# Down projection of a gated FFN in seven block products, with earlier loads at two places ahead of it

## The chip, the cores and the metric

The kernel runs on one core of a Trainium2 chip. The metric is device time in microseconds, from one launch. The core has TensorE (matmul, "PE"; its weight loads are "PEld"), VectorE ("DVE"), ScalarE ("ACT"), GpSimd ("POOL") and SyncE ("SP", used for starting DMAs); "SPq", "ACTq" and "POOLq" are DMA issues on those engines' queues.

## The reference

One decoder layer on x of 1024 tokens by 1024 features, float32:

```
h = rmsnorm(x, norm_mix_g);  z = h @ w_in            # 1024 x 2816
y_a: short gated conv; y_b: attention, 8 heads of 64; y_c: Conformer conv (31 taps), layernorm, silu
x = x + concat(rmsnorm(y_a), rmsnorm(y_b), rmsnorm(y_c)) @ w_out
h = rmsnorm(x, norm_ffn_g)
gate, val = split(causal_dwconv(h @ w_up, conv_f_w, 3 taps))   # 2 x 2816 features
x = x + (silu(gate) * val) @ w_down                  # (1024 x 2816) @ (2816 x 1024)
return rmsnorm(x, final_g)
```

## The kernel before

Every float32 operand of a matmul is split into a rounded part `hi` (ACT copy, line 71) and a rest `lo` (a subtraction on DVE or POOL, line 72). A product is three matmuls, hi*hi, hi*lo, lo*hi (`mm3`, lines 89 to 92: L90, L91, L92), each 128x128 by 128x512. The order of TensorE's instructions is the program order, written by hand; the other engines' instructions are put in an order by the framework's planner ahead of the run, and wait on semaphores. Each engine and each DMA queue then works in that order.

The stages, in order of time:

- Front: projections of the input. `proj_qk(i, ...)` makes a 128-row block of queries (i below 4) or keys (i = 4 to 7), splits it and stores hi and lo to DRAM (`qk[i]`). Blocks 0, 4, 1, 5 are made here.
- Attention (about 235 to 445 us): 80 chunks, ten for each of 8 heads. `load_head(h)` brings a head's query, key, bias and value tiles from DRAM, most of it on POOL's queue; heads 0 and 1 are loaded after the last projection, the others one or two heads ahead. Between the attention's matmuls TensorE runs "filler" from a generator: `more_qk()` (blocks 2, 6, 3, 7, tile `f_ps`), then `out_ac()`, the part of the output projection that doesn't need attention. `out_ac()` starts with `yield 0` four times while the splits `yh`/`yl` of its activations are made, then loads the weights of the first 512 columns into tiles `wac` and the residual x on ACT's queue.
- Out projection, norm, up projection (about 530 to 929 us). The up projection already works by seven block products instead of eight: weight sums are made on POOL (L971 to L974), one loop per 128 gate and 128 value features (`main(j)`, 22 loops). Each loop stores its activations, a 128 x 1024 block (features by tokens), to DRAM as `actd[j]` (L1007). After loops 19 and 20 `early_tiles` splits the first two blocks for the down projection into the tiles of `b11` and `b21`, which are free by then.
- Down projection (from 929 us): two halves of 512 tokens; for each, 22 blocks `kt` of 128 features, and in each block 8 output banks by three matmuls. The weights `w_down[kt]` (512 KB) are loaded and split anew in each half (`wd_hi`, `wd_lo`), the activations (256 KB) are loaded from `actd` and split (`a_hi`, `a_lo`). The last three blocks of a half run bank by bank (LAG = 3), so that each bank's residual add (L1098), square (L1100) and final norm (`finish`) overlap the next bank's matmuls.

Of the kernel before, what the change touches and what calls it, by code (L numbers as in the profile page):

```python
# [36 lines left out]
def body(tc, x_t, x_n, grow, par, cst, rel, oneh, nlnc, wc, w_cols, wv, w_out, w_up, w_down, out):  # L37
# [345 lines left out]

    def proj_qk(i, pos, tmp=None):
# [11 lines left out]
        split(t[:, :S], hi, lo, G if tmp else V)  # L396
        nc.sync.dma_start(out=qk[i][0], in_=f(hi))
# [78 lines left out]
    do_norm()  # L476
    table(AF.Exp, "sqrt")
# [9 lines left out]

    def load_head(h):
        j, s = h // 2, (h % 2) * 64
        sa = a0.tile([P, S], F32R, name="sa", tag="sa", bufs=2)  # L490
        sb = a0.tile([P, S], F32R, name="sb", tag="sb", bufs=2)
        sm = a0.tile([P, S], F32R, name="sm", tag="sm", bufs=2)
        g = a0.tile([P, S], F32, name="g", tag="g", bufs=2)
        vv = a0.tile([P, TT, P], F32R, name="vv", tag="vv", bufs=2)
        for dst, src in ((sa, (qk[j][0], qk[j][0])), (sb, (qk[j][1], qk[j][1])), (sm, (qk[4 + j][0], qk[4 + j][1]))):
            for e in range(2):
                G.dma_start(out=dst[e * 64:(e + 1) * 64, :], in_=src[e][s:s + 64, :])
        fr = fs[h:h + 1, 1:1 + S]
# [17 lines left out]
    heads = {0: load_head(0), 1: load_head(1)}  # L516
# [115 lines left out]

    yh, yl = [None] * 8, [None] * 8
# [4 lines left out]
    def load_half(rows, dh, hi, lo):  # L638
# [5 lines left out]
        mark["w"] = split(raw, hi, lo, G)  # L644
# [13 lines left out]
    def out_ac():  # L658

        close(c_x)  # L660
# [41 lines left out]
        for q in range(2):  # L702
            load_row(4 + q, *wp_pair())
# [259 lines left out]
    def main(j):  # L963
# [43 lines left out]
        nc.sync.dma_start(out=actd[j], in_=cg)  # L1007
# [158 lines left out]
```

## Time and profile before

| what | value |
|---|---|
| median of 3 runs | 1184.74 us (1183.36 to 1184.91) |
| the profiled execution | 1181.71 us, of it 1179.9 us from the first to the last instruction |
| granted TensorE clock, mean | 0.984 of full speed |
| PE, PEld, DVE, ACT, POOL busy | 96%, 80%, 64%, 43%, 44% of the span |
| attention, 235 to 445 us | 210 us |
| down projection, 929 to 1173 us | 244 us |

Busy time counts a pipelined matmul from its start to its modelled end, so two matmuls overlap: a matmul's listed duration is longer than the pace at which matmuls follow each other. The pace is read as a stretch divided by the matmuls in it. The granted clock is a share of 2.4 GHz.

### The profile page before, as it was taken

The numbers are of one execution on the slowest core, as the hardware profiler recorded it, in microseconds if no ns is written. First come the engines' busy times: TensorE is split into PE (matmuls) and PEld (weight loads), VectorE is DVE, ScalarE is ACT, GpSimd is POOL, SyncE is SP. The second block draws the span as 40 slices with busy tenths as digits, with TensorE's granted clock in tenths as the row PEclk, the third lists the DMA queues.
The fourth block names the chain that finished last, engine by engine and source line by source line (L and its number), as shares of the span: only waits on it lengthen the run. The fifth ranks groups of instructions, "written<-read, shape, count | busy, mean of one in ns | idle before, by whom it ended". The sixth has DMA issues, their size and how long they took to land.

```text
span 1179.9 us, 14291 instructions
## 1 busy us (share of the span) xinstructions
PE 1138.5 (96%) x5327; PEld 943.7 (80%) x5327; DVE 757.4 (64%) x886; ACT 503.7 (43%) x798; POOL 521.3 (44%) x328
## 2 busy tenths in 40 slices
PE   9999979899979999989999999999999999999997
PEld 7888868788858887868888888888887788888886
DVE  7599965356656666796677887788778722164214
ACT  7212115256555655573444444444444432343323
POOL 4223522423222203036677777777776043334331
PEclk9999989999989999989999999999999999999999
DMA  6218214977689604223242342332423554456531
GB/s 239 86 40 234 73 53 121 309 195 166 156 236 228 143 1 161 96 102 124 78 138 89 108 141 83 133 108 90 142 89 126 169 191 158 146 188 217 171 116 72
DMA packets 59317, 162.80 MB, mean 138 GB/s; under 512 B 6232, under 2 KB 15952, under 8 KB 59248
## 3 DMA queue, kind: packets, MB, share of 16 engines
q1 hardware_dynamic: 44784, 139.27, 36.1%
q0 software_dynamic: 12160, 16.78, 7.2%
q10 hardware_dynamic: 2304, 5.83, 1.4%
q8 instruction: 42, 0.69, 0.3%
q14 instruction: 27, 0.22, 0.1%
HBM read 127.17 MB, written 34.69 MB: 137 GB/s over the span
## 4 chain that ended last, share of the span: by engine, by line
PE 83%; DVE 6%; DMA 5%; ACT 3%; issue 2%; POOL 1%; SPq 0%; ACTq 0%; DVEq 0%; POOLq 0%
PE cb L91 8%; PE cb L90 8%; PE cb L92 8%; PE d_ps L92 7%; PE d_ps L91 6%; PE d_ps L90 6%; PE ca L92 4%; PE ca L90 4%; PE ca L91 4%; PE pv_ps L581 2%; PE f_ps L90 2%; PE f_ps L92 2%; PE f_ps L91 2%; PE t_ps L550 2%; PE v L92 1%
## 5 line engine op out<-in xcount | busy, mean ns | idle before, releaser
L72 POOL TENSOR_TENSOR w_lo<-w_raw,w_hi 128x1024 fp32r<-128x1024 f32 (+2 forms) x49 | 108.7, 2220 | 204.6 <-ACT w_hi L71 204.6
L960 DVE SCALAR_TENSOR_TENSOR x<-ut,pr,x 128x1024 f32<-128x1024 f32 x88 | 147.0, 1688 | 18.8 <-ACT x L958 18.0
L72 POOL TENSOR_TENSOR wd_lo<-w_raw,wd_hi 128x1024 fp32r<-128x1024 f32 x32 | 78.4, 2454 | 163.3 <-ACT wd_hi L71 150.7
L92 PE MATMUL d_ps<-wd_hi,a_lo 128*128 128x512 f32 x336 | 131.7, 392 | 1.2 <-DVE a_lo L72 1.2
L90 PE MATMUL d_ps<-wd_hi,a_hi 128*128 128x512 f32 x336 | 131.5, 391 | 0.5 <-ACT a_hi L71 0.5
L91 PE MATMUL d_ps<-wd_lo,a_hi 128*128 128x512 f32 x336 | 131.4, 391 | 0.5 <-POOL wd_lo L72 0.5
L72 DVE TENSOR_TENSOR a_lo<-a_raw,a_hi 128x512 fp32r<-128x512 f32 x42 | 40.0, 961 | 132.4 <-ACT a_hi L71 125.3
L71 ACT CAST w_hi<-w_raw 128x512 fp32r<-128x512 f32 (+2 forms) x61 | 46.1, 764 | 138.8 <-PE v L92 23.6
L298 DVE SCALAR_TENSOR_TENSOR yc<-u,pr,yc 128x1024 f32<-128x1024 f32 x60 | 89.7, 1548 | 1.7 <-ACT yc L295 1.4
L92 PEld LDWEIGHTS d_ps<-wd_hi,a_lo 128*128 128x128 f32 x336 | 63.5, 189 | 14.6 <-DVE a_lo L72 1.5
L90 PEld LDWEIGHTS d_ps<-wd_hi,a_hi 128*128 128x128 f32 x336 | 63.5, 189 | 14.2 <-ACT a_hi L71 1.0
L91 PEld LDWEIGHTS d_ps<-wd_lo,a_hi 128*128 128x128 f32 x336 | 63.4, 189 | 13.9 <-POOL wd_lo L72 0.8
L71 ACT CAST a_hi<-a_raw 128x512 fp32r<-128x512 f32 x42 | 25.8, 620 | 111.9 <-PE d_ps L91 108.6
L958 ACT ACTIVATE x<-ut,pr 128x1024 f32<-128x1024 f32 x44 | 50.7, 1153 | 47.8 <-DVE ut L1000 32.6
L537 ACT ACTIVATE p<-p,mn 128x128 f32<-128x128 f32 (+3 forms) x64 | 49.8, 778 | 40.5 <-DVE mn L534 40.3
L1006 DVE TENSOR_TENSOR x<-x 128x1024 f32<-128x1024 f32 x22 | 46.3, 2105 | 10.6 <-ACT x L1005 10.6
L71 ACT CAST wd_hi<-w_raw 128x1024 fp32r<-128x1024 f32 x42 | 43.9, 1048 | 20.0 <-DMA w_raw<-in 20.0
L997 DVE TENSOR_TENSOR ut<-cb,yb 128x512 f32<-128x512 f32 x22 | 15.2, 690 | 56.3 <-PE cb L92 56.3
L561 DVE TENSOR_TENSOR ptl<-t_ps,pth 128x512 fp32r<-128x512 f32 x48 | 33.1, 690 | 20.6 <-ACT pth L560 20.1
L971 POOL TENSOR_TENSOR xp<-xp 128x512 f32<-128x512 f32 x11 | 21.2, 1925 | 55.2 <-DMA xp<-in 49.8
L550 PE MATMUL t_ps<-ident,p 128*128 128x128 f32 x288 | 44.4, 272 | 0.0
L534 DVE CUSTOM_DVE_ANT_0 p<-l_ps,g 128x640 f32<-128x640 f32 (+5 forms) x34 | 33.8, 995 | 15.0 <-PE l_ps L528 14.4
(405 smaller groups left out, 3319.1 us busy)
## 6 DMA issues: line engine op xcount, KB each, us to landing
w_raw<-in SPq DMA_DIRECT2D x93, 512.0 KB, 3.7
ur<-in SPq DMA_DIRECT2D x22, 512.0 KB, 3.7
xp<-in SPq DMA_DIRECT2D x22, 512.0 KB
actd<-x SPq DMA_DIRECT2D x22, 512.0 KB
a_raw<-actd SPq DMA_DIRECT2D x42, 256.0 KB, 2.8
vd<-vt SPq DMA_DIRECT2D x8, 512.0 KB
vv<-vd POOLq DMA_DIRECT2D x8, 512.0 KB, 5.4
g<-fs SPq DMA_DIRECT2D x8, 512.0 KB, 9.5
```

Of the source, the lines that this page charges most:

```text
L71: cp = A.copy(hi, src)
L72: lo_eng.tensor_tensor(out=lo, in0=src, in1=f(hi), op=ALU.subtract)
L90: T.matmul(ps, whi, xhi, start=start, stop=False, **kw)
L91: T.matmul(ps, whi, xlo, start=False, stop=False, **kw)
L92: T.matmul(ps, wlo, xhi, start=False, stop=stop, **kw)
L298: V.scalar_tensor_tensor(out=yc[i], in0=u[i][:, j:j + S], scalar=col("cwc", j * 2 + i), in1=yc[i], op0=ALU.mult, op1=ALU.add)
L534: V.tensor_tensor_reduce(out=p[:, :n], in0=ps[:, :n], in1=gq, op0=ALU.add, op1=ALU.min, scale=1.0, scalar=3e38, accum_out=mn[:, ix:ix + 1])
L537: mark["exp"] = A.activation(out=p[:, :n], in_=p[:, :n], func=AF.Exp, scale=-1.0, bias=mn[:, ix:ix + 1], accum_out=den[h // 2][:, dc:dc + 1])
L550: T.transpose(out=tp[:, i * P:(i + 1) * P], in_=p[:, kj * P:(kj + 1) * P], identity=ident)
L958: A.activation(out=c, in_=t[:, 2:], func=AF.Copy, scale=col("cwf", 2 * 44 + m))
L960: V.scalar_tensor_tensor(out=c, in0=t[:, q:q + S], scalar=col("cwf", q * 44 + m), in1=c, op0=ALU.mult, op1=ALU.add)
L1006: V.tensor_tensor(out=cg, in0=cg, in1=cv, op=ALU.mult)
```

## The change

The down projection C = A B (tokens x 2816, 2816 x 1024) is cut into 2 x 2 blocks: A by 512 tokens and 1408 features, B by 1408 features and 512 columns. Seven products of 11 feature blocks and 4 banks replace the eight. Sums of weights (T1 = B12 - B11, T3 = B22 - B12, T2 = B22 - T1) are made on POOL inside the attention, 11 times three subtractions, and stored to DRAM. Sums of activations S1 = A21 + A22 and S2 = S1 - A11 are loaded on POOL's queue, made on POOL and DVE, and stay in SBUF. Three operands are made as a product needs them, on POOL: A11 - A21 (P7), A12 - S2 (P3), T2 - B21 (P4). P1, P2 share banks x, P5, P3 share banks y. Four early blocks are made instead of two. Ahead of it: query block 0 and key block 4 stay in SBUF (not stored), and heads 0 and 1 are loaded ahead of the last front projection; the first weights of `out_ac` go into the pair of weight tiles and are asked for before the wait for the input's tiles; x comes on SP's queue. The step numbers in `SAT` and `XAT` count feature blocks, 11 to a product. `done2`, `done6`, `done7` and `done3` add a bank to the residual x3 or to a partial sum, and `done3` finishes tokens 0 to 511. The diff, cut:

```diff
+    def load_head(h):
...
+        q, k = qk[j], qk[4 + j]
+        for dst, src in ((sa, (q[0], q[0])), (sb, (q[1], q[1])), (sm, (k[0], k[1]))):
+            for e in range(2):
+                G.dma_start(out=dst[e * 64:(e + 1) * 64, :], in_=src[e][s:s + 64, :])
...
     def proj_qk(i, pos, tmp=None):
...
+        if i % 4 == 0:
+            qk[i] = hi, lo
+            return
         nc.sync.dma_start(out=qk[i][0], in_=f(hi))
...
     proj_qk(1, 9)
     do_norm()
+    heads = {0: load_head(0), 1: load_head(1)}
     table(AF.Exp, "sqrt")
     proj_qk(5, 10, (yb[2], yb[3].bitcast(F32R), yb[2].bitcast(F32R)))
...
-    heads = {0: load_head(0), 1: load_head(1)}
...
+    def weights_load(i):
+        x = tw if i < 4 else [a1.tile([P, 512], F32, name=n, tag=n, bufs=1) for n in TW]
+        for t, (r, q) in zip(x, ((i, 0), (i, 1), (i + HF, 1))):
+            nc.sync.dma_start(out=t, in_=w_down[r * P:(r + 1) * P, q * 512:q * 512 + 512])
+    def weights_add(i):
+        b11, b12, b22 = twt.pop(i)
+        G.tensor_tensor(out=b11, in0=b12, in1=b11, op=ALU.subtract)
+        G.tensor_tensor(out=b12, in0=b22, in1=b12, op=ALU.subtract)
+        G.tensor_tensor(out=b22, in0=b22, in1=b11, op=ALU.subtract)
+        for n, t in (("T1", b11), ("T3", b12), ("T2", b22)):
+            nc.sync.dma_start(out=tsum[n][i], in_=t)
...
     def out_ac():
-        close(c_x)
+        w2 = [wp_pair() for _ in range(2)]
+        for q, r in enumerate((0, 6)):
+            load_half(r, 0, *w2[q])
+        close(c_tw, c_x)
...
-                        for q in ((0, 1) if t == 0 else (t + 1,) if t < 7 else ()):
-                            nc.scalar.dma_start(out=xp2[q], in_=x_n[q * P:(q + 1) * P, :])
+                if dh == 0 and t < 6:
+                    nc.sync.dma_start(out=xp2[t + 2], in_=x_n[(t + 2) * P:(t + 3) * P, :])
...
+    TWAT = (3, 12, 21, 30, 43, 48, 53, 58, 63, 68, 73)
+        if i in TWAT:
+            weights_load(TWAT.index(i))
+        elif i - 2 in TWAT:
+            weights_add(TWAT.index(i - 2))
...
+    SRC = {"P1": ((A11,), (B11,)), "P2": ((A12,), (B21,)), "P6": ((S2,), (T2,)), "P7": ((A11, A21), (T3,)),
+           "P5": ((S1,), (T1,)), "P3": ((A12, S2), (B22,)), "P4": ((A22,), (T2, B21))}
...
+            for q in range(2):
+                early[2 * (j - FT + 3) + q] = early_tiles(2 * (j - FT + 3) + q)
...
+    def sums_load(i):
+        for x, spec in ((ss_[S1][i], A21), (t, A22), (ss_[S2][i], A11)):
+            G.dma_start(out=x, in_=quadrant(spec, i))
+    def sums_add(i, t):
+        G.tensor_tensor(out=s1, in0=s1, in1=t, op=ALU.add)
+        V.tensor_tensor(out=s2, in0=s1, in1=s2, op=ALU.subtract)
+    def down_tiles(n, kt):
...
+                    x[i] = dn.tile([P, 512], F32, name=f"{e}_raw{i}", tag=f"{e}_raw{i}", bufs=NBUF if i == 0 else 2)
+                    nc.sync.dma_start(out=x[i], in_=quadrant(spec, kt))
...
+            if len(x) > 1:
+                G.tensor_tensor(out=raw, in0=raw, in1=x[1], op=ALU.subtract)
+            split(raw, hi, lo, V)
...
+    XAT = (6, 10, 15, 19, 45, 46, 47, 48)
+    SAT = (5, 8, 11, 14, 17, 20, 22, 24, 26, 27, 28)
+    ORDER = ("P1", "P2", "P6", "P7", "P5", "P3", "P4")
+    def run(n, y, done):
+        lag = LAG if n == "P4" else 1
...
+            ops = tiles[kt] = early[kt] if n == "P1" and kt in early else down_tiles(n, kt)
+            if kt < HF - lag:
+                for t in range(4):
+                    dmm(n, y, t, kt, ops, n not in start_of)
         for t in range(4):
...
+            for kt in range(HF - lag, HF):
+                dmm(n, y, t, kt, tiles[kt], n not in start_of)
+            done(t, banks[n, t])
...
+    def done1(t, ps):
+        A.copy(p1[t], ps)
...
+    def done5(t, ps):
+        for q in HS:
+            tt(x3[4 + t][:, q], x3[4 + t][:, q], u3[t])
+        tt(x3[4 + t][:, HS[1]], ps, x3[4 + t][:, HS[1]])
+        square(4 + t, 1)
...
+    def done4(t, ps):
+        x, o = x3[4 + t], xo[t % 2]
+        if t == 3:
+            tt(o[:, HS[1]], x[:, HS[1]], gfrow[:, HS[1]], ALU.mult, G)
+        tt(x[:, HS[0]], x[:, HS[0]], ps, ALU.subtract)
+        square(4 + t, 0)
+        finish(4 + t, o if t == 3 else None)
```

## Rows read from the trace of the kernel before

**Rows 1.** Page, busy time: us, share of the span, instructions.

```profile
PE 1138.5 (96%) x5327; PEld 943.7 (80%) x5327; DVE 757.4 (64%) x886; ACT 503.7 (43%) x798; POOL 521.3 (44%) x328
```

**Rows 2.** Windows: length, busy us (xinstructions) by engine, granted clock, DMA share, GB/s.

```profile
227.00:236.00 9.00, 4.85 (x17) 3.87 (x16) 3.00 (x10) 3.19 (x6) 4.66 (x2) 0.81 1.05 339
338.00:351.00 13.00, 6.36 (x22) 4.79 (x21) 3.68 (x6) 5.21 (x9) 5.65 (x3) 0.61 0.75 244
348.00:362.00 14.00, 13.02 (x66) 10.91 (x65) 7.12 (x11) 5.56 (x10) 6.33 (x8) 0.89 1.11 387
235.00:445.00 210.00, 198.81 (x1171) 169.87 (x1169) 130.19 (x256) 118.68 (x240) 56.59 (x60) 0.98 0.64 160
560.00:900.00 340.00, 340.00 (x1502) 281.71 (x1501) 259.37 (x228) 153.41 (x217) 254.44 (x155) 1.00 0.34 112
1060.00:1160.00 100.00, 100.00 (x443) 82.85 (x442) 26.65 (x26) 30.12 (x39) 34.39 (x14) 1.00 0.48 156
```

**Rows 3.** Waits of TensorE over the span: us in total, times, longest.

```profile
PE f_ps L90 <- ACT wac_hi L71: 5.0, 1, 5.0
...
PE f_ps L91 <- POOL wac_lo L72: 1.6, 1, 1.6
...
PE d_ps L92 <- DVE a_lo L72: 1.2, 1, 1.2
```

**Rows 4.** Timeline of TensorE at three places: start, us, instruction [idle before, releaser].

```profile
231.46 0.36 PE L527 MATMUL s_ps<-sm,sa 128*128 128x256 f32 x1 [4.15 <-DMA sm<-qk]
...
343.95 0.80 PE L90 MATMUL f_ps<-wac_hi,yh 128*128 128x512 f32 x1 [5.02 <-ACT wac_hi L71]
...
346.96 0.63 PE L92 MATMUL f_ps<-wac_hi,yl 128*128 128x512 f32 x1
...
350.80 0.57 PE L90 MATMUL f_ps<-wac_hi,yh 128*128 128x512 f32 x1
...
938.26 0.39 PE L92 MATMUL d_ps<-b21h,b21l 128*128 128x512 f32 x1
939.19 0.50 PE L90 MATMUL d_ps<-wd_hi,a_hi 128*128 128x512 f32 x1 [0.54 <-ACT a_hi L71]
...
945.29 0.39 PE L91 MATMUL d_ps<-wd_lo,a_hi 128*128 128x512 f32 x1
```

**Rows 5.** Tile `d_ps`: instructions, ns min/median/max, first and last start.

```profile
L90 PE MATMUL d_ps<-wd_hi,a_hi x336: 388/389/629, 939.2 to 1172.2; 128*128 128x512 f32 x168
```

**Rows 6.** Timelines of SP's queue and of POOL at the two places ahead.

```profile
223.78 2.27 POOL L497 DMA_DIRECT2D sm<-qk  x4 [3.98 <-DMA qk<-q_hi]
...
338.63 10.83 SPq L641 DMA_DIRECT2D w_raw<-in  x4
```

**Rows 7.** Groups by line and form: count, busy us, mean ns, idle before.

```profile
L72 DVE TENSOR_TENSOR a_lo<-a_raw,a_hi 128x512 fp32r<-128x512 f32 x42 | 40.0, 961 | 132.4 <-ACT a_hi L71 125.3 <-PE d_ps L91 3.7 <-DMA w_raw<-in 3.3
...
L71 ACT CAST a_hi<-a_raw 128x512 fp32r<-128x512 f32 x42 | 25.8, 620 | 111.9 <-PE d_ps L91 108.6 <-issue 3.3
```

**Rows 8.** Timelines of POOL and DVE, alone and side by side.

```profile
612.64 1.30 POOL L72 TENSOR_TENSOR w_lo<-ur,w_hi 128x512 fp32r<-128x512 f32 x1
613.89 2.28 POOL L72 TENSOR_TENSOR w_lo<-xp,w_hi 128x512 fp32r<-128x512 f32 x1
...
612.65 2.37 DVE L1006 TENSOR_TENSOR x<-x 128x1024 f32<-128x1024 f32 x1 [0.53 <-ACT x L1005]
...
947.63 4.76 POOL L72 TENSOR_TENSOR wd_lo<-w_raw,wd_hi 128x1024 fp32r<-128x1024 f32 x2 [7.50 <-ACT wd_hi L71]
...
950.49 2.45 DVE L72 TENSOR_TENSOR a_lo<-a_raw,a_hi 128x512 fp32r<-128x512 f32 x1 [6.87 <-ACT a_hi L71]
...
1010.33 0.69 DVE L72 TENSOR_TENSOR a_lo<-a_raw,a_hi 128x512 fp32r<-128x512 f32 x1 [4.75 <-ACT a_hi L71]
```

**Rows 9.** Timeline of the last 7 us.

```profile
1173.10 0.69 DVE L1098 TENSOR_TENSOR x<-d_ps,x 128x512 f32<-128x512 f32 x1
```

**Rows 10.** Page, DMA queues: packets, MB, share of 16 engines.

```profile
q0 software_dynamic: 12160, 16.78, 7.2%
```

More of the change, by code (lines that the diff above doesn't have):

```diff
@@ L643, in load_half @@
                           .rearrange("(b p) c -> p b c", b=2))
-        mark["w"] = split(raw, hi, lo, G)
+        for q in range(2):
+            q = slice(q * 512, q * 512 + 512)
+            mark["w"] = split(raw[:, q], hi[:, q], lo[:, q], G)
     def load_row(k, hi, lo):
@@ L1021, in body @@
         if j in (FT - 3, FT - 2):
-            early[j - FT + 3] = early_tiles(j - FT + 3)
-    close(c_um, c_h2, held["xp"], c_y, c_mm)
+            for q in range(2):
+                early[2 * (j - FT + 3) + q] = early_tiles(2 * (j - FT + 3) + q)
+    close(c_um, c_h2, held["xp"], c_y, c_w, c_mm)
     c_dn, dn = pool("dn", "left")
@@ L1051, in finish, with square @@
+    def square(t, dh):
+        q = HS[dh]
+        A.activation(out=xo[t % 2][:, q], in_=x3[t][:, q], func=AF.Square,
+                     accum_out=s3[:, 2 * t + dh:2 * t + dh + 1])
     def finish(t, last):
-        x, c = x3[t % 4], slice(t, t + 1)
+        x, c = x3[t], slice(t, t + 1)
         r = s3[:, 16:][:, c]
@@ L1058, in finish @@
         V.reciprocal(out=r, in_=r)
-        for q in HS if last else (slice(0, D),):
-            if last and q == HS[0]:
+        for q in HS if last is not None else (slice(0, D),):
+            if last is not None and q == HS[1]:
                 A.activation(out=x[:, q], in_=last[:, q], func=AF.Copy, scale=r)
@@ L1105, in body, with dmm @@
-    close(c_dp, c_dn, c_h, c_w, c_pad, c_const, c_dr)
+    nc.sync.dma_start(out=gfrow, in_=grow[1:2, :].broadcast_to([P, D]))
+    banks = {}
+    def dmm(n, y, t, kt, ops, start=True):
+        if (n, t) not in banks:
+            banks[n, t] = dps.tile([P, 512], F32, name=f"d_{y}{t}", tag=f"d_{y}{t}") if start else banks[start_of[n], t]
+        ah, al, bh, bl = ops
+        ts = slice(t * P, (t + 1) * P)
+        mm3(banks[n, t], ah[:, ts], al[:, ts], bh, bl, start and kt == 0, kt == HF - 1,
+            **({} if start else {"skip_group_check": True}))
@@ new lines, in done3 @@
+    def done3(t, ps):
+        tt(x3[t][:, HS[1]], ps, x3[t][:, HS[1]])
+        square(t, 1)
+        finish(t, None)
+    def done4(t, ps):
[5 more added lines that the diff above has]
+        finish(4 + t, o if t == 3 else None)
+    run("P1", "x", done1)
+    run("P2", "x", done2)
+    run("P6", "y", done6)
+    run("P7", "x", done7)
@@ L1106, in body @@
+    run("P5", "y", done5)
+    run("P3", "y", done3)
+    run("P4", "x", done4)
+    close(c_dp, c_dn, c_h, c_pad, c_const, c_dr)
     ms.__exit__(None, None, None)
```

171 lines of the change are left out of this document (89 added, 82 removed).

## Prediction

> **What bounds the kernel now.** I read the page's busy line first: TensorE is busy for 96% of the span, every other engine for 64% or less [rows 1]. Then the windows, to see stretch by stretch whether TensorE runs without a break. In the up projection, 560 to 900 us, it is busy for 340 of 340 us at full granted clock, 1502 matmuls, 226.4 ns each; in the down projection, 1060 to 1160, 443 in 100 us, 225.7 ns [rows 2]. Some records can be missing, so I take the pace from neighbouring starts, 0.227 us (three matmuls 0.68). So there the number of matmuls is the time. Then TensorE's list of waits, for the places where it isn't. Three places touch the change [rows 3, 4]:
>
> A, from about 339 us: the first matmul of `out_ac` waits 5.0 us for `wac_hi`, the next 1.6 for `wac_lo`. After them the matmuls follow at half pace: from 346.96 to 350.80 [rows 4], while the granted clock of 338 to 351 is 0.61 [rows 2].
>
> B, 227.3 us: the first score of the attention waits 4.15 us for the DMA of head 0's keys [rows 4], and the window 227 to 236 has a clock of 0.81 [rows 2].
>
> C, 938.5 us: the first non-early block of the down projection. The last early matmul starts at 938.26, so the next was due at 938.49; it starts at 939.19, the list of waits has 1.2 us behind it for `a_lo`, and at 945.29, ten matmuls on, the pace is back [rows 3, 4].
>
> **The change part by part.** The sum is made against the profiled execution, 1181.71 us, 1.8 of them outside the span.
>
> *Matmuls.* Before: 22 blocks x 16 banks x 3 = 1056, which the tile view confirms: 336 in each of the three operations [rows 5], and two early blocks of 8 x 3 under other tile names. After: 7 products x 11 blocks x 4 banks x 3 = 924. 132 fewer by 0.2267 us: **-29.9 us**. Nothing can hide this: TensorE has no gap there [rows 2].
>
> *C, the start.* Ten matmuls take from 939.19 to 945.29, 6.1 us instead of 2.3, and start 0.7 late: 4.5 us lost [rows 4]. Four early blocks hold 48 matmuls instead of 42, which moves the need for the next block from 938.5 to 939.9. Its splits are two of 512 columns per block (ACT 0.62, DVE 0.69 each [rows 7, 8]) where one of 1024 stood. They can still come late by an engine's order, so between 0 and -4.5; I take **-3.5**, as the need comes later and the chain is shorter.
>
> *B.* Lost: 4.2 waiting, and at most 0.19 x 9 = 1.7 of clock [rows 2], 5.9 in all. POOL's four key loads are issued at 223.78, after waiting 4.0 for key block 4 to land in DRAM [rows 6], and 7.7 us later, at 231.46, the score starts [rows 4]. Without the DRAM trip the keys can be asked for when the split is done, some 7 us earlier. Next late would be the last projection's readers or the score's chain on DVE and ACT. Between -2 and -6; I take **-5**.
>
> *A.* Lost: 5.0 + 1.6 + about 2.5 at half clock (3.84 us of matmuls that would take 1.9, and two starting slow) = 9.1. The load of the weights is issued only at 338.63 [rows 6], since its raw buffers held inputs of the `yh` splits. After the change weights come first; then the fourth `yh` input is what can be late, as it now waits for a raw buffer. It is needed nine matmuls behind the first. Between -5 and -9; **-7.5**.
>
> *Sums of weights.* 33 subtractions of 128x512 at 1.30 [rows 8] = 43 us of POOL, 33 loads and 33 stores of 256 KB on SP's queue. POOL is busy 57 of 210 us in the attention, and the DMAs carry 160 GB/s [rows 2]; 17.3 MB more in 210 us add 82. DVE's work there reads mostly PSUM. Behind a POOL subtraction stand the `f_lo` splits and the head loads, a head and more ahead of use. Cover: POOL's 153 idle us; without it, up to 43. Between 0 and +4; **+0.5**.
>
> *Within the products.* A block lasts 12 x 0.2267 = 2.72 us. ACT: two splits, 1.24. DVE: two, 1.38. POOL in P7, P3 and P4: one subtraction, 1.30. Each engine has room, but DVE and POOL don't run side by side: an `a_lo` takes 0.69 alone and 2.45 beside POOL's pair of 947.63; in the up projection POOL's 1.30, DVE's 1024-column operation and another POOL one end 3.53 us after the first began (612.64 to 616.17), almost one after another [rows 8]. Laid end to end that is 1.30 + 1.38 = 2.68 of 2.72. It fits, as it does in the up projection, where both engines are busy about 255 of 340 us each and TensorE never stops [rows 2]. Four buffers let the splits run three blocks ahead, 8 us. The Trainium skill (GPSIMD Engine Reference, "Key points") says that GpSimd shares its SBUF interfaces with VectorE and contends with two-input operations; by full exclusion the three products have 2.68 of 2.72, with nothing over for the final norms in P4, which is the second rival; the trace agrees that the two take turns.
>
> DMA: quarter tiles of 0.262 MB. P1 14 (four early blocks are done), P2 22, P6 11, P7 33, P5 11, P3 22, P4 33: 146, and 33 for the activation sums; with x3 and the output 4.2 MB each, 55.3 MB in 209.5 us = 264 GB/s, against 156 before [rows 2]. The heaviest stretch is steps 4 to 28: 43 tile loads, 33 for sums, 4 of x3 (8 tiles' worth): 22.0 MB in 68 us = 324 GB/s. The trace carried 387 GB/s for 14 us [rows 2]; so it fits too, with little over. The Trainium skill (DMA: Bandwidth & Descriptors, "Issuing engines are not separate DMA queues") says that POOL's queue brings no further DMA engines; by it the 324 is one demand, as I have counted it, and no row here tests it.
>
> Boundaries: P2 overwrites P1's banks after ACT's copies, P3 adds to P5's after DVE's reads; nine matmuls, 2.0 us, lie between. A gap like C costs 4.5 with its slow clock. From 0 (the stretch 1060 to 1160 behind the change of halves runs whole) to 13.5 (three such gaps); I take **+3**, less than one.
>
> *Tail.* The last banks of P4 come every nine matmuls (2.04 us) where two took 4.08, and DVE has 0.69 for each [rows 9] plus some 1.7 for the norm: 2.4 per token block. Three blocks fall behind by 0.4: **+1** (0 to 2).
>
> Sum: -29.9 - 3.5 - 5 - 7.5 + 0.5 + 3 + 1 = **-41.4**: 1140.3. The profiled run lies 3.0 under the median of the runs shown, so 1143.3; I say **1143**. Ends: all gains whole and no cost, -29.9 - 4.5 - 6 - 9 = -49.4, 1135; with C, B and A at their small ends, two gaps and the tail at 2, -29.9 - 2 - 5 + 0.5 + 9 + 2 = -25.4, 1159.
>
> **Rivals.**
>
> 1. *The places ahead give nothing.* POOL's queue is in order; if its head loads or the fourth `yh` input are late again, A and B stay. For it: the wait on POOL in [rows 6]. Against: the DRAM trip and the late raw buffer are gone. -41.4 + 12.5 = -28.9: about 1156.
>
> 2. *DVE and POOL become the bound.* If each of the 33 blocks of P7, P3 and P4 takes POOL 1.30 and DVE twice its mean of 0.96 [rows 7], 3.22 instead of 2.72, +16.5; with POOL at 2.28 and DVE at 0.69, 3.66, +31. For it: 2.68 of 2.72 is nearly all. Against: the up projection. 1143 - 3 + 16.5 to + 31: 1157 to 1171.
>
> 3. *Slower: DMA becomes the bound.* POOL's queue moved 16.78 MB in 7.2% of 1179.9 us, 197 GB/s [rows 10]. If the stage as a whole ran at that rate, its 55.3 MB take 281 us instead of 212.5: 1143 + 68 = 1211. It decides where the rate stays under 218 GB/s (55.3 MB in 254 us). Against: 387 GB/s [rows 2].
>
> **How the numbers follow.** Forecast 0.68 (1135 to 1152), rival 1 0.12, rival 2 0.13, rival 3 0.04, something faster than all terms 0.03. Range 1134 to 1163: the forecast, rival 1 and the lower part of rival 2. A measurement of this kernel tells about 0.2%, 2.4 us, from no change. Faster: all but rival 3 and a scrap of the rest, 0.94; same 0.02; slower 0.04.
>
> **What would show it.** Right: about 924 matmuls on the down banks at 0.227; from the first to the last of them about 212 us; no wait of TensorE over 1 us at the first score and the first `out_ac` matmul, with the clock near 1.0 there; attention's other stretches as long as before. Wrong: waits of TensorE on `a_lo`, `b_lo` in P7, P3 or P4 with DVE operations of 2 us (rival 2); casts waiting for DMAs in P1 and P2, or a granted clock under 0.9 in a product (rival 3); the first score still waiting for keys (rival 1); waits on T stores or `f_lo` in the attention.

## The result and the profile after

The changed kernel takes 1192.5 us (median of 8 runs), the kernel before 1183.3 in the same session: a ratio of 1.0064, 95% interval 1.0042 to 1.0086. It is slower by 0.6%, where 1143 was forecast. The profiled execution took 1193.07 us, 1191.3 of them in the span.

The page's busy line and its chain of work that ended last, of the kernel after [rows 1]:

```profile
PE 1117.9 (94%) x5195; PEld 922.1 (77%) x5195; DVE 837.1 (70%) x1015; ACT 525.0 (44%) x872; POOL 576.7 (48%) x418
...
PE 69%; DMA 16%; DVE 7%; ACT 3%; issue 2%; POOL 2%; SPq 1%; ACTq 0%; DVEq 0%; POOLq 0%
```

There are 132 matmuls fewer, as counted, and TensorE's busy share fell. The chain now runs through DMAs for 16% of the span, 5% before. TensorE's list of waits, the longest that touch the change (total, times, longest) [rows 3]:

```profile
PE l_ps L531 <- DVE mn L538: 10.6, 3, 5.5
PE d_x L90 <- ACT b_hi L71: 10.6, 5, 7.6
PE cb L884 <- DVE b22l L72: 8.9, 1, 8.9
...
PE d_x L91 <- DVE b_lo L72: 5.4, 7, 2.1
PE tr_ps L137 <- DVE st_c L128: 4.1, 2, 3.6
```

Five lines, four places, for which the sum had +0.5 (the attention), +3 (the two in the down projection) and nothing (the fourth). To see which stage lost how much I take TensorE's timeline and read the start of the same five matmuls in every run: the first score, the first of `out_ac`, the last transpose of token block 7, the first and the last of the down projection. From here on a stage is the difference of two columns (us from the start of the profiled span). Medians are of all runs; the one of experiment 7 holds one execution of 3076.7 us, without which it is 1184.2. The starts belong to the profiled execution alone, whose own time stands in the second column: it lies 4.8 above the median in experiment 4 and 7.0 below it in experiment 10, so the starts of two kernels can differ by some us without an edit behind it.

| kernel | median | profiled | first score | `out_ac` | last transpose | down, first | down, last |
|---|---|---|---|---|---|---|---|
| before | 1183.3 | 1181.7 | 231.5 | 344.0 | 518.7 | 929.0 | 1172.7 |
| after | 1192.5 | 1193.1 | 233.4 | 354.6 | 537.0 | 949.0 | 1182.5 |
| e1 no weight sums | 1168.4 | 1172.7 | 233.5 | 340.4 | 516.6 | 929.5 | 1162.1 |
| e2 paced | 1175.0 | 1175.6 | 234.5 | 354.5 | 534.5 | 944.7 | 1164.7 |
| e3 norms spread | 1187.2 | 1184.1 | 231.9 | 355.3 | 534.4 | 946.0 | 1173.6 |
| e4 front only | 1178.3 | 1183.1 | 231.3 | 337.1 | 519.8 | 930.1 | 1173.9 |
| e5 sums' DMAs on POOL | 1175.2 | 1173.1 | 233.9 | 338.7 | 522.7 | 932.7 | 1162.5 |
| e6 sums in up projection | 1208.9 | 1208.5 | 232.8 | 338.6 | 517.9 | 968.4 | 1197.7 |
| e7 DVE's order | 1184.3 | 1180.3 | 226.7 | 345.7 | 524.0 | 938.0 | 1169.8 |
| e8 all, sums in up | 1195.8 | 1194.4 | 227.0 | 333.5 | 506.2 | 965.5 | 1183.5 |
| e9 all, sums' DMAs on POOL | 1158.6 | 1157.1 | 227.8 | 337.4 | 512.9 | 929.0 | 1146.6 |
| e10 paced on POOL | 1180.2 | 1173.3 | 229.9 | 349.2 | 531.5 | 942.1 | 1162.7 |
| e11 front, DVE's order | 1172.9 | 1172.5 | 226.5 | 333.5 | 508.6 | 921.1 | 1163.3 |
| e12 e9, sums earlier | 1160.1 | 1163.1 | 225.8 | 333.1 | 515.2 | 933.7 | 1152.6 |

So the changed kernel enters the down projection 20.0 us late instead of 12.0 early, and needs 233.5 us for it, where 924 matmuls at 0.2267 are 209.5 and the kernel before needed 243.7. There are four places.

**In the attention**, 275 to 312 us. Rows of the timeline of the kernel after, of SP, ACT, DVE and PE:

```profile
275.91 4.13 SPq L658 DMA_DIRECT2D T<-tw  x3
280.14 3.61 SPq L649 DMA_DIRECT2D tw<-in  x3
283.84 0.39 SPq L633 DMA_DIRECT2D qk<-f_hi  x1
...
291.85 0.39 SPq L142 DMA_DIRECT2D scr<-tr_r  x1
...
295.38 0.32 SPq L658 DMA_DIRECT2D T<-tw  x1
295.79 0.52 SPq L633 DMA_DIRECT2D qk<-f_hi  x1
300.16 1.15 SPq L601 DMA_DIRECT2D rden<-scr  x2
...
304.89 0.62 ACT L71 CAST f_hi<-f_t 128x512 fp32r<-128x512 f32 x1 [6.23 <-DMA qk<-f_hi]
308.38 1.23 DVE L606 TENSOR_TENSOR yb<-yb,rden 128x1024 f32<-128x1024 f32 x1 [7.43 <-DMA rden<-scr]
311.26 0.79 PE L531 MATMUL l_ps<-sm,sa 128*128 128x512 f32 x1 [5.46 <-DVE mn L538]
```

It is read from the bottom. TensorE waits 5.46 for DVE's minimum; DVE had stood 7.43 in front of the product with `rden`. `rden` (the denominators of the softmax, spread over the partitions) goes through DRAM: DVE had written its rows at 284.2, SP issued their store at 291.85, behind stores of T that wait for POOL's subtractions and loads of `tw` that wait for those stores, and the load at 300.16, when that store had landed. ACT stands 6.23 for the store of the last `f_hi`, which is in the same queue, with the next exponentials behind it.

**In the first two products**, 949 to 1010. The windows of the kernel after [rows 2]:

```profile
949.00:980.00 31.00, 23.43 (x100) 18.80 (x99) 12.74 (x16) 9.54 (x15) 13.67 (x25) 0.89 0.83 302
978.50:984.00 5.50, 5.50 (x13) 3.80 (x13) 3.61 (x4) 1.68 (x3) 3.51 (x6) 0.57 1.04 389
980.00:1010.00 30.00, 26.38 (x103) 19.64 (x102) 18.54 (x22) 15.68 (x26) 13.77 (x18) 0.95 1.02 378
...
1070.00:1100.00 30.00, 30.00 (x134) 24.84 (x133) 24.73 (x35) 12.66 (x22) 8.66 (x6) 1.00 0.53 168
```

A stretch of 30 us at full pace has 134 matmuls, as the last line shows. 949 to 1010 has 203 of the 269 that fit into 61 us: 15 us lost. Half of it is one wait, 7.6 us up to 978.5; behind it the granted clock was 0.57 for 5.5 us, in which 13 matmuls ran, about 2.5 us more than at the pace. The timeline of the same kernel shows who is late:

```profile
959.21 0.32 SPq L1114 DMA_DIRECT2D a_raw<-actd  x1
959.74 0.54 POOL L1099 DMA_DIRECT2D S<-actd  x1 [7.60 <-DVE a_lo L72]
960.80 2.13 POOL L1099 DMA_DIRECT2D S<-actd  x4
...
970.11 0.33 SPq L1114 DMA_DIRECT2D b_raw<-in  x1
970.60 0.54 POOL L1099 DMA_DIRECT2D S<-actd  x1 [0.49 <-DMA S<-actd]
...
977.83 0.62 ACT L71 CAST b_hi<-b_raw 128x512 fp32r<-128x512 f32 x1 [7.06 <-DMA b_raw<-in]
978.50 0.80 PE L90 MATMUL d_x<-b_hi,a_hi 128*128 128x512 f32 x1 [7.57 <-ACT b_hi L71]
```

POOL has nothing that makes it wait for the products, so it issues loads for sums of later steps as fast as earlier ones land, and the quarter of w_down that TensorE needs next, issued at 970.11, is split 7.7 us later.

**In the last product**, 1151 to 1175. The timeline of the kernel after:

```profile
1151.20 7.96 DVE L1141 SCALAR_TENSOR_TENSOR x<-x,s,gfrow 128x1024 f32<-128x1024 f32 x4
...
1160.75 1.70 SPq L1142 DMA_DIRECT2D out_dram<-x  x2
1161.49 0.50 PE L91 MATMUL d_x<-b_lo,a_hi 128*128 128x512 f32 x1 [2.09 <-DVE b_lo L72]
1162.54 1.16 SPq L1114 DMA_DIRECT2D a_raw<-actd  x1
1168.51 0.62 ACT L71 CAST a_hi<-a_raw 128x512 fp32r<-128x512 f32 x1 [7.57 <-DMA a_raw<-actd]
```

The four norms of token blocks 0 to 3, which P3 ends, stand on DVE in one piece, 8 us beside POOL's subtractions. The splits come behind them, and SP, which waits for the norms with their output, issues the last loads behind 2 MB of output.

**At 207 and 526 us** (in the kernel before, and in the texts below, 202 and 507), in lines that the diff doesn't touch: `tr_ps` waits 3.6 for `st_c`, `cb` 8.9 for `b22l`. In the kernel before, the waits of `cb` there come to 4.1, none of them for `b22l`. The order that the planner gave DVE is another one at both (experiments 4 and 7). At 526 a norm stands in front of the split that TensorE waits for, as DVE's timeline of the kernel after shows:

```profile
523.03 2.28 DVE L872 SCALAR_TENSOR_TENSOR xp<-xp,rcol,g2row 128x1024 f32<-128x1024 f32 x1
525.24 0.68 DVE L72 TENSOR_TENSOR b22l<-cb,b22h 128x512 fp32r<-128x512 f32 x1
```

### The profile page after: what moved, and what is told of

Same layout as the page of the kernel before. It is cut to its first block, busy times and chain, and to the rows that moved or that the text cites. A ratio compares the mean times of both kernels' runs of the same rounds, so it can differ in the third digit from the quotient of the medians.

```text
span 1191.3 us, 14741 instructions
## 1 busy us (share of the span) xinstructions
PE 1117.9 (94%) x5195; PEld 922.1 (77%) x5195; DVE 837.1 (70%) x1015; ACT 525.0 (44%) x872; POOL 576.7 (48%) x418
## 4 chain that ended last, share of the span: by engine, by line
PE 69%; DMA 16%; DVE 7%; ACT 3%; issue 2%; POOL 2%; SPq 1%; ACTq 0%; DVEq 0%; POOLq 0%
PE cb L90 8%; PE cb L91 8%; PE cb L92 8%; PE ca L92 4%; PE ca L90 4%; PE ca L91 4%; DMA b_raw<-in 2%; PE d_y L90 2%; PE d_y L91 2%; PE d_y L92 2%; DMA scr<-tr_r 2%; PE d_x L91 2%; PE d_x L92 2%; PE d_x L90 2%; DMA f_lo<-in 1%
## 5 line engine op out<-in xcount | busy, mean ns | idle before, releaser
L72 POOL TENSOR_TENSOR w_lo<-w_raw,w_hi 128x512 fp32r<-128x512 f32 (+2 forms) x51 | 107.9, 2120 | 160.4 <-ACT w_hi L71 160.3
L90 PE MATMUL d_x<-b_hi,a_hi 128*128 128x512 f32 x160 | 64.3, 402 | 10.6 <-ACT b_hi L71 10.6
L72 DVE TENSOR_TENSOR b_lo<-b_raw,b_hi 128x512 fp32r<-128x512 f32 x73 | 60.3, 826 | 16.9 <-ACT b_hi L71 16.9
L91 PE MATMUL d_x<-b_lo,a_hi 128*128 128x512 f32 x160 | 64.7, 404 | 5.4 <-DVE b_lo L72 5.4
L92 PE MATMUL d_x<-b_hi,a_lo 128*128 128x512 f32 x160 | 63.5, 397 | 0.0
L71 ACT CAST b_hi<-b_raw 128x512 fp32r<-128x512 f32 x73 | 45.0, 616 | 20.4 <-DMA b_raw<-in 15.0
L90 PE MATMUL d_y<-b_hi,a_hi 128*128 128x512 f32 x132 | 51.5, 390 | 0.7 <-DVE x L1187 0.7
L91 PE MATMUL d_y<-b_lo,a_hi 128*128 128x512 f32 x132 | 51.4, 389 | 0.0
L92 PE MATMUL d_y<-b_hi,a_lo 128*128 128x512 f32 x132 | 51.4, 389 | 0.0
L90 PEld LDWEIGHTS d_x<-b_hi,a_hi 128*128 128x128 f32 x160 | 30.9, 193 | 19.2 <-ACT b_hi L71 12.7
```

Of the source, the lines that this page charges most:

```text
L71: cp = A.copy(hi, src)
L72: lo_eng.tensor_tensor(out=lo, in0=src, in1=f(hi), op=ALU.subtract)
L90: T.matmul(ps, whi, xhi, start=start, stop=False, **kw)
L91: T.matmul(ps, whi, xlo, start=False, stop=False, **kw)
L92: T.matmul(ps, wlo, xhi, start=False, stop=stop, **kw)
```

## The experiments

**1. Without the weight sums.** The down projection reads quarters of w_down where T1 to T3 stood, so the output isn't the reference's.

```diff
-        if i in TWAT:
-            weights_load(TWAT.index(i))
-        elif i - 2 in TWAT:
-            weights_add(TWAT.index(i - 2))
...
-    T1, T2, T3 = ((tsum[n], 0, 0) for n in ("T1", "T2", "T3"))
+    T1, T2, T3 = (w_down, 0, 0), (w_down, HF, 0), (w_down, 0, 1)
```

> Leaves out the sums of weights: no loads, subtractions or stores of T in the attention; the down projection reads quarters of w_down where it read T1 to T3, so its transfers and its arithmetic stay in number, and the output is not the reference's. Theory 1 (the T traffic stands in SP's in-order queue in front of the stores and loads that the attention waits for, f_hi and rden): the delays that the changed kernel gathers at 274 to 337 us (16 us) and at 407 (3.7) go, 20 us: about 1173, with TensorE's waits for mn and t_ps under 2 us each. Rival (the order that the planner gave DVE and the early weights of out_ac cause them): under 5 us, 1188 or more.

1168.4 us, ratio to before 0.9879 (0.9856 to 0.9903): 24 us less than the changed kernel. From the first score to the first down matmul it takes 696.0 us instead of 715.6. The down projection is as long as before the edit, 232.6. So the sums, put at +0.5, cost about 20 where they are made.

**2. The down projection's other loads paced by SP.**

```diff
-        for x, spec in ((ss_[S1][i], A21), (t, A22), (ss_[S2][i], A11)):
-            G.dma_start(out=x, in_=quadrant(spec, i))
+        with tc.issue_after(mark["ld"].ins):
+            for x, spec in ((ss_[S1][i], A21), (t, A22), (ss_[S2][i], A11)):
+                nc.sync.dma_start(out=x, in_=quadrant(spec, i))
...
-                G.dma_start(out=x3[t], in_=x2d[t])
+                with tc.issue_after(mark["ld"].ins):
+                    nc.sync.dma_start(out=x3[t], in_=x2d[t])
...
-                    nc.sync.dma_start(out=x[i], in_=quadrant(spec, kt))
+                    mark["ld"] = nc.sync.dma_start(out=x[i], in_=quadrant(spec, kt))
```

> The 33 loads for the activation sums and the eight of x3 are issued by SP, each behind the tile load of its step, instead of by POOL's queue. Theory 1 (POOL's queue runs ahead of its steps and takes DMA bandwidth from the tile loads of the first two products, which lose 15 us from 949 to 1010): 12 to 15 us less, about 1178; the window 949 to 980 over 130 matmuls instead of 100, no wait of TensorE over 2 us there. Rival 1 (the DMAs as a whole are the bound in steps 0 to 28): under 4 us less, with the waits moved to later steps. Rival 2 (the sums, now later, hold up the third product): slower, with waits of a_hi for S2.

1175.0 us, ratio 0.9929 (0.9912 to 0.9946). The down projection takes 220.0 instead of 233.5; the other 4 us of the medians' difference lie ahead of it, where nothing was edited. The windows of this kernel for the same 61 us of the stage:

```profile
944.70:975.70 31.00, 29.00 (x123) 22.39 (x122) 17.92 (x22) 12.19 (x18) 3.49 (x3) 1.00 0.72 259
975.70:1005.70 30.00, 28.93 (x125) 23.45 (x126) 19.65 (x28) 16.86 (x29) 7.85 (x6) 1.00 1.05 388
```

248 matmuls instead of 203; the first window has 123, where over 130 were expected. The second stretch moves 388 GB/s and TensorE hardly waits; in the first the DMAs carry less than before the edit, 259 instead of 302. The quarters of w_down that TensorE needs next now land sooner (issues of the stretch, the last number is the median time to landing in us). In the kernel after, 949 to 1010:

```profile
b_raw<-in SPq DMA_DIRECT2D x16, 256.0 KB, 11.5
```

and here, 944.7 to 1005.7:

```profile
b_raw<-in SPq DMA_DIRECT2D x19, 256.0 KB, 5.3
```

Each load is as large as before, and what counts is which of them goes first. Both rivals fall. The edit changes the queue and the moment at once; experiment 10 parts them.

**3. The norms spread, their output behind the last loads.**

```diff
 def done3(t, ps):
     ...
-    finish(t, None)
...
+            if n == "P4" and 4 <= kt < 8:
+                with tc.issue_after(mark["lo"].ins):
+                    finish(kt - 4, None)
+            if n == "P4" and kt == HF - 1:
+                with tc.issue_after(mark["ld"].ins):
+                    for t in range(4):
+                        nc.sync.dma_start(out=out[t * P:(t + 1) * P, :], in_=x3[t])
```

> The four norms of token blocks 0 to 3 stand on DVE behind the splits of blocks 4, 5, 6 and 7 of the last product instead of all four in front of block 4, and their output stores behind that product's last tile loads on SP. Theory 1 (four norms in a row, 8 us of DVE, and 2 MB of output in front of the last loads make TensorE wait at 1161 to 1175): 6 to 8 us less, about 1185.5. Rival (DVE and POOL taking turns make the last product late wherever the norms stand): within 2 us of the changed kernel's 1192.5, with waits for b_lo or b_hi moved earlier in the product.

1187.2 us, ratio 1.0023 (1.0000 to 1.0045); the down projection takes 227.5, 6.0 less. TensorE's longest wait for `b_lo` fell from 2.1 to 0.6. In the last product DVE and POOL do as many operations as before, so it wasn't their sum that was too long but an order: DVE's, or that of SP's queue. The edit moves the norms and their output together, and no run parts the two.

**4. The front alone.** The kernel before, with the diff's hunks for `load_head`, `proj_qk`, `load_half` and `out_ac`, without T, and with the old down projection.

```diff
+        if i % 4 == 0:
+            qk[i] = hi, lo
+            return
...
+    heads = {0: load_head(0), 1: load_head(1)}
     table(AF.Exp, "sqrt")
...
+        w2 = [wp_pair() for _ in range(2)]
+        for q, r in enumerate((0, 6)):
+            load_half(r, 0, *w2[q])
         close(c_x)
```

> The kernel before with the changes in front of the down projection alone: the keys and queries of blocks 0 and 4 from SBUF, load_head earlier, out_ac's weights ahead of its inputs; no sums of weights, the old down projection. Theory 1 (these edits give 4.3 us at the first score and 7.4 less 2.9 at out_ac, as the trace after shows): 9 us less than before, about 1174.5. Rival (they also move the planner's order on DVE, which costs 3.8 at 202 us and 6 at 507): about 1183 to 1185, no gain.

1178.3 us, ratio 0.9958 (0.9943 to 0.9972): 5 less, between the two. `out_ac` starts at 337.1 instead of 344.0, and yet the down projection starts at 930.1; this execution is 4.8 slower than the median, so part of that is its own. The waits at 202 and 507 are in this kernel too, 3.8 and 7.8 us, so they belong to the front. DVE's timeline at 202, of this kernel:

```profile
202.22 1.28 DVE L458 SCALAR_TENSOR_TENSOR yb<-yb,pr,gn_a 128x1024 f32<-128x1024 f32 x1 [3.32 <-DMA gn_a<-scr]
203.42 0.16 DVE L125 TENSOR_SCALAR st_c<-st_ps 128x8 f32<-128x8 f32 x1
```

and of the kernel before:

```profile
200.26 0.15 DVE L125 TENSOR_SCALAR st_c<-st_ps 128x8 f32<-128x8 f32 x1
...
203.26 2.48 DVE L438 SCALAR_TENSOR_TENSOR yb<-yb,pr,gn_a 128x1024 f32<-128x1024 f32 x2 [2.37 <-DMA gn_a<-scr]
```

The planner put the norm first; `gn_a` landed 3.3 us late, and the statistic that TensorE waits for stood behind it. Two stores of queries no longer stand on SP there; whether that is why the planner chose so, no trace shows.

**5. The weight sums' DMAs on POOL's queue.**

```diff
-            nc.sync.dma_start(out=t, in_=w_down[r * P:(r + 1) * P, q * 512:q * 512 + 512])
+            G.dma_start(out=t, in_=w_down[r * P:(r + 1) * P, q * 512:q * 512 + 512])
...
-            nc.sync.dma_start(out=tsum[n][i], in_=t)
+            G.dma_start(out=tsum[n][i], in_=t)
```

> The loads and stores of the weight sums are issued by POOL's queue instead of SP's; sums, places and bytes are the same. Theory 1 (the loss in the attention is the order of SP's queue: stores of T that wait for POOL stand in front of f_hi's and rden's transfers): most of the 24 us that leaving the sums out gave comes back, 1172 to 1177, and DVE's wait for rden and ACT's for f_hi fall under 2 us. Rival (the loss is the bandwidth of the transfers themselves, whoever issues them): within 5 us of 1192.5. Second rival (POOL, now in order behind loads that land late, holds up f_lo and the head loads): 1185 or slower, with waits of PE on keys or values.

1175.2 us, ratio 0.9937 (0.9917 to 0.9956): 17 of the 24 us come back with the same sums and the same bytes. First score to down: 698.9 us, against 715.6 on SP's queue and 696.0 without sums. Neither list of waits has the one of ACT for `qk<-f_hi` or the one of DVE for `rden<-scr` any more. POOL's timeline in this kernel:

```profile
408.72 0.54 POOL L649 DMA_DIRECT2D f_t<-in  x1
410.24 0.54 POOL L649 DMA_DIRECT2D f_hi<-in  x1 [0.98 <-DMA T<-f_hi]
411.47 0.54 POOL L649 DMA_DIRECT2D f_lo<-in  x1 [0.69 <-DMA T<-f_lo]
413.66 1.29 POOL L654 TENSOR_TENSOR f_t<-f_hi,f_t 128x512 f32<-128x512 f32 x1 [1.65 <-DMA f_hi<-in]
```

The same waits are now POOL's. 66 issues at 0.54 cost it 36 us, which it has; the `f_lo` splits and the head loads stand behind them, and no matmul waits over 0.6 us for one. The bandwidth was not the matter, as the windows of the attention show. In the kernel after:

```profile
235.00:445.00 210.00, 188.57 (x1090) 160.10 (x1089) 121.65 (x246) 111.86 (x236) 97.19 (x94) 0.98 0.89 239
```

and in this one:

```profile
235.00:445.00 210.00, 200.18 (x1185) 170.72 (x1183) 136.23 (x264) 125.32 (x255) 132.07 (x154) 0.99 0.89 239
```

Both carry 239 GB/s at a DMA share of 0.89, and this one fits 95 matmuls more into the same time. Both rivals fall. The Trainium skill (DMA: Bandwidth & Descriptors, "Issuing engines are not separate DMA queues") says that to issue from several engines saves no more than the sequencer's time; here it saved 17 us, by what no longer stood behind a waiting transfer.

**6. The weight sums in the up projection.** One in every second step, its loads behind that step's on SP, its sums behind the step's on POOL, in the free halves of `xp2[6]` and `xp2[7]`.

```diff
-        if i in TWAT:
-            weights_load(TWAT.index(i))
-        elif i - 2 in TWAT:
-            weights_add(TWAT.index(i - 2))
...
         main(j)
+        if j % 2 == 0:
+            if j:
+                weights_store(j // 2 - 1)
+            weights_load(j // 2)
+        else:
+            weights_add(j // 2)
```

> The sums of weights are made in the up projection, one of the eleven in every second step, each part pinned behind that step's loads on SP and its sums on POOL; buffers are free halves of the residual tiles. Theory 1 (what costs is the place: in the up projection the DMAs have room, and 43 us of POOL fit beside its 255 of 340): the attention is as in the run without sums, the up projection stays at its pace: 1168 to 1172. Rival (POOL and DVE take turns there, 43 us more make TensorE wait): the attention's 24 us come back, and 10 to 30 us go in the up projection: 1178 to 1198.

1208.9 us, ratio 1.0239 (1.0199 to 1.0280), worse than the rival's range. From the first score to the last transpose it takes 18.5 us less than the changed kernel, and from the last transpose to the down projection it takes 450.6 us instead of 412.0. A window of this kernel, where TensorE has 233 of the 265 matmuls that fit, and two of TensorE's waits:

```profile
680.00:740.00 60.00, 54.79 (x233) 44.31 (x232) 48.35 (x36) 23.04 (x34) 54.72 (x31) 0.97 0.35 114
```

```profile
PE ca L92 <- POOL so_lo L72: 7.6, 4, 3.9
PE ca L92 <- POOL w_lo L72: 5.8, 3, 3.9
```

33 subtractions, 43 us by the 1.30 of one that is alone, lost 39; beside DVE's work thirty of them take 2.1 each. POOL is busy for 55 of 60 us there, and TensorE waits for its splits. That POOL's time is the whole cause isn't shown: POOL also stands 52 us for loads of w_up in this stage, 40 in the kernel after, and these share SP's queue with the sums' transfers.

**7. DVE's two orders written out.**

```diff
     proj_qk(4, 8)
-    do_norm()
+    with tc.issue_after(mark["rec"].ins):
+        do_norm()
...
             A.copy(q1, bk[0])
-            put("t2", t2)
             V.tensor_tensor(out=q1, in0=bk[1], in1=q1, op=ALU.subtract)
             put("b22", bk[1])
+        with tc.issue_after(mark["lo"].ins):
+            if t == 4:
+                ob_norm(7)
+            put("t2", t2)
             put("t3", q1)
```

> Two orders on DVE are written out: the small statistic in front of the norm that waits for gn_a, and in the transposing of token blocks 4 to 7 the operations that release a PSUM bank in front of the others and of the last norm. Theory 1 (the changed front let the planner choose an order on DVE that costs 3.8 us at 202 and 6 at 507): 8 to 10 us less than the changed kernel, about 1183; no wait of tr_ps for st_c over 1 us, cb's wait for b22l under 3. Rival (what is late there is the DMA, and TensorE waits as long for another operation): within 2 us of 1192.5.

1184.3 us, ratio 1.0008 (0.9986 to 1.0030): 8 less than the changed kernel. The first score comes at 226.7 instead of 233.4; 202 is mended whole. At 507 TensorE waits 3.7 for `b22l` instead of 8.9 (under 3 was expected), and 1.4 for `t2l` comes in its place: from `out_ac` to the down projection it takes 592.3 instead of 594.4, 2 us.

**8. Paced, norms spread, orders, and the sums in the up projection** (the edits of 2, 3, 6 and 7).

> All of it together: the down projection's loads paced by SP, the norms spread, the sums of weights in the up projection, DVE's two orders written out. Theory 1 (the places are apart from each other and their losses add): 1192.5 less 17.5 (paced, measured), 5.3 (norms, measured), 22 (no sums in the attention, near the 24 measured) and 8 (the orders) is about 1140, within 4 us of the 1143 forecast. Rival (one loss only moves to the next bound, DVE and POOL by turns): 1155 to 1165.

1195.8 us, ratio 1.0116 (1.0085 to 1.0147), far from both the 1140 of the theory and the rival's 1155 to 1165. The down projection takes 218.0 us; the up projection takes back more than was gained, as in experiment 6 (last transpose to down 459.3).

**9. The edits of 2, 3, 5 and 7 together.**

> Four mends together: the weight sums' transfers on POOL's queue in the attention, the down projection's loads paced by SP, the norms spread, DVE's two orders written out. Theory 1 (four places, losses that add): 1192.5 less 17.3 (transfers on POOL's queue), 17.5 (paced), 5.3 (norms) and 8 (orders), each as measured alone, is about 1144, the time forecast for the change, with no wait of TensorE over 3 us in the places named. Rival (some of the losses covered each other, so that they don't add): 1152 or more.

1158.6 us, ratio 0.9800 (0.9768 to 0.9832): 34 us less than the changed kernel, 25 less than before, and some 14 more than the sum of the four said. The down projection takes 217.6, 8.1 over 209.5, with 122 and 124 matmuls in its first 31 and 30 us, as in experiment 2. The time is in the rival's range: the gains don't add. Of the missing 14, experiment 2's median held 4 us that lie ahead of its edit, and the gains of 2 and 3 inside the down projection come to 15.9 together, not 13.5 + 6.0 = 19.5. Another 4 lie between the last transpose and the down projection, 416.1 us here, 412.0 after and 410.3 before: at 526 TensorE waits 1.1 for `t2h` and 1.4 for `t2l`, which experiment 7's order put behind `b22` (the kernels with that order, 7, 9, 11 and 12, all have the 1.4, the kernel after has none). The rest was not settled.

**10. Paced, but on POOL's queue.**

```diff
+            mark["st"] = G.tensor_copy(probe, f(ops[0][:, :1]))
...
-        for x, spec in ((ss_[S1][i], A21), (t, A22), (ss_[S2][i], A11)):
-            G.dma_start(out=x, in_=quadrant(spec, i))
+        with tc.issue_after(mark["st"].ins):
+            for x, spec in ((ss_[S1][i], A21), (t, A22), (ss_[S2][i], A11)):
+                G.dma_start(out=x, in_=quadrant(spec, i))
```

> Parts two things that the paced run changed at once, the queue and the moment: the activation sums' and x3's loads stay on POOL's queue, but each stands behind a copy of one column of the step's hi tile on POOL, so that POOL can't run ahead of the tiles. Theory 1 (the moment is what counts): 12 to 17 us less than the changed kernel's 1192.5, like the paced run's 1175. Rival (POOL's queue itself is what slows the tile loads): within 4 us of 1192.5. Second rival (POOL, now waiting for tiles, makes its sums too late for the third product): slower, with waits for S.

1180.2 us, ratio 0.9963 (0.9940 to 0.9987), 12 less than the changed kernel; the profiled execution took 1173.3, and in it the down projection takes 220.6, as with SP's queue (220.0). Its first 61 us in this kernel's windows:

```profile
942.10:973.10 31.00, 29.61 (x129) 23.84 (x128) 17.33 (x23) 14.05 (x22) 12.74 (x21) 1.00 0.74 264
973.10:1003.10 30.00, 30.00 (x134) 24.83 (x133) 19.09 (x28) 15.88 (x28) 21.78 (x36) 1.00 1.03 383
```

A copy of one column that POOL has to wait for is enough: in the first two products it was the moment, not the queue. The second rival comes in by a little: in the third product the casts of `a_hi` wait 10.0 us in all for DVE's part of the sums, and 115 matmuls run in 30 us. The median is 5 us above experiment 2's, and where the slower executions lose that, no trace shows.

**11. The front alone, with DVE's orders** (the edits of 4 and 7).

> The kernel before with the changed front alone (as in the run that had 1178.3) and DVE's two orders written out. Theory 1 (the front's gains at the first score and at out_ac were given back at 202 and 507 by the order): 8 us less than that run, about 1170, that is 12.5 less than before, which is what the prediction's places A and B came to. Rival (the orders cost nothing where no weight sums are made): 1177 to 1180.

1172.9 us, ratio 0.9917 (0.9898 to 0.9936): 5 less than experiment 4. The down projection starts at 921.1, 7.9 ahead of before. So the front's places give 11 by the medians, where 12.5 was forecast, once the order is kept (7.9 at the start of the down projection in the profiled execution, 2.2 having gone behind the last transpose), and the seven products as in experiment 9 are worth another 14.

**12. Experiment 9, the weight sums begun earlier.**

```diff
-    TWAT = (3, 12, 21, 30, 43, 48, 53, 58, 63, 68, 73)
+    TWAT = (3, 12, 21, 30, 40, 43, 46, 50, 54, 58, 62)
```

> The run with the four mends, and the last seven of the eleven weight sums begun up to eleven chunks earlier, so that they end before DVE's yl splits at 439 us, which take 5.8 us for three beside POOL's subtractions, and PE waits 2.3 there. Theory (the sums' tail on POOL slows those splits): about 2 us less than the 1158.6 of that run, 1156 to 1157. Rival (packed closer, the sums hold up the head loads on POOL's queue): 1159 to 1165, with waits of PE on keys or values between 340 and 430.

1160.1 us, ratio 0.9799 (0.9779 to 0.9819), no gain. The time is in the rival's range, but its sign, waits for keys or values, didn't come. The edit missed its aim: each sum waits for its own transfers, so the last ones end where they did (stores of T until 457 and 458 us), and the `yl` splits got slower: three of them take 5.83 in experiment 9. DVE's timeline in experiment 11, without sums:

```profile
436.52 3.67 DVE L75 SCALAR_TENSOR_TENSOR yl<-yb,pr,yh 128x1024 fp32r<-128x1024 f32 x3
```

and the timeline of experiment 12:

```profile
435.44 2.40 POOL L72 TENSOR_TENSOR wac_lo<-w_raw,wac_hi 128x1024 fp32r<-128x1024 f32 x1
436.83 8.58 DVE L75 SCALAR_TENSOR_TENSOR yl<-yb,pr,yh 128x1024 fp32r<-128x1024 f32 x3
437.79 1.27 POOL L657 TENSOR_TENSOR f_lo<-f_lo,f_t 128x512 f32<-128x512 f32 x1
439.58 2.35 POOL L72 TENSOR_TENSOR wac_lo<-w_raw,wac_hi 128x1024 fp32r<-128x1024 f32 x1
```

8.58 is the 3.67 and the 1.0, 1.27 and 2.35 of POOL in between, and a little more: one after another. The Trainium skill (GPSIMD Engine Reference, "Key points") says that the two share their interfaces to SBUF and contend where DVE has two inputs there; the trace agrees.

## Why the prediction was wrong

**Matmuls, right.** 132 fewer, at the pace forecast: 134 in each 30 us from 1010 to 1100. The 29.9 us are there (924 by 0.2267 instead of 1056); everything else together took 41.

**Places B, A and C, right in size.** The first score gained 4.3 (5 taken): in experiment 11 it comes at 226.5, 4.9 earlier, some of that ahead of it. `out_ac`'s two waits gained 7.4, read along the aligned matmuls of the two traces (5.3 at its first matmul, 2.1 at the second); the fourth `yh` then came 2.2 late in the kernel after, which the working had named and not priced. Over the thirty matmuls behind the last one ahead of the wait, 15.1 us before and 8.7 after, the gain is 6.4 of the 7.5 taken. Experiment 11 as a whole is 11 less than before; A and B were put at 12.5. At the start of the down projection nothing was lost: no gap over half a us from 949 to 970.

**Sums of weights: the step that failed first.** "Cover: POOL's 153 idle us": I looked for the cover of the arithmetic, and the cost was in the transfers' place. The 66 DMAs stand on SP's in-order queue, each store behind a subtraction, each load behind a store, and what stands behind them there (`f_hi`'s stores with one buffer, `rden`) is needed by ACT and DVE. +0.5 was taken, 0 to +4 as bounds; about 20 was measured (experiments 1 and 5). The last part of the prediction named "waits on T stores", but no rival had them.

**Within the products: the step that failed next.** +3 was taken, 0 to +13.5, for gaps at the boundaries. Where TensorE's matmuls start over half a us apart, the stage loses 20.5 us against the pace, 14 of them in the first two products and 6 in the last; at the boundaries one gap of 0.9 is left. I had set the mean demand, 324 GB/s, against the 387 that the trace showed, and it does fit: experiment 2 runs the same loads with a third of the loss (21 matmuls missing in 61 us instead of 66). What the mean doesn't show is that POOL's queue spends its loads early, since nothing on POOL waits for the products. The sign set for the third rival did come, casts that wait 7 us for DMAs in the first product and a granted clock of 0.89 in its window; the rival itself (DMA as the bound of the stage) isn't what happened: 1010 to 1100 runs whole, and the loads fit once they are paced. So the sign didn't part a bound from an order.

**DVE and POOL by turns (rival 2)** did not decide in the products that I had named: the fourth (P7, from about 1055) runs at full pace beside POOL's subtractions, the sixth (P3, from about 1115) with one gap of 0.9 us. It was right as a mechanism: the four norms, beside POOL's operations, take 8 us, and in the up projection experiment 6 found little room left.

**Not seen at all**: that an edit moves the planner's order in lines that it doesn't touch. Two places, 3.8 and about 5 us, took back most of what A and B gave (experiments 4, 7 and 11).

In all: start to first score 6.9 worse than forecast (3.6 of it the wait at 207; the rest lies in the front, where the kernels with this front and the planner's order have their first score anywhere from 229.9 to 234.5), from there to the first down matmul some 25, down 20, tail 0.6; that is the 53 us between 1140.3 and the profiled 1193.07. The change itself is sound: with its transfers where they stand in nobody's way, the norms spread and DVE's orders written out it takes 1158.6 us (experiment 9), 15.6 us from the stated 1143 and inside the range.

## What to carry to other kernels

Cost a moved or added transfer by its queue: what its issue waits for, and who needs what stands behind it there; idle time of an engine covers arithmetic, not the order of a queue. A queue whose engine waits for nothing in a stage issues its loads as early as buffers and earlier loads let it, so tie loads for later steps to the steps, on whichever queue. And where a planner orders the instructions, compare each engine's order with that of the kernel before at once: it shows losses in lines that the diff doesn't touch.

## What the runs showed of the hardware

- One column copied by POOL in every step, a wait and next to no work, paced its loads as well as another queue did: 220.6 against 220.0 us for the stage in the profiled executions.
- The DMAs carried 383 GB/s over 30 us (experiment 10, share 1.03) with TensorE whole, 134 matmuls, and 388 (experiment 2, share 1.05) with 125; the same loads issued earlier, at 302 and 378 GB/s, lost 15 us in 61, and a quarter of w_down took 11.5 us to land instead of 5.3.
- Three splits of 1024 columns on DVE take 3.67 us alone and 8.58 beside three operations of POOL. In the up projection, where POOL was busy for 47 of 60 us (680 to 740), 33 more subtractions with their transfers cost 39 us of the span.
